# Third buffers for the first table and the rows, an eight-step pause and a larger side budget in the expert stage of a hybrid mLSTM, S5 and PEER block

## The chip, the cores and the metric

The kernel runs on one core of one Trainium2 chip. The metric is the device time of one execution in microseconds. Engines are PE (TensorE, matrix products), DVE (VectorE), ACT (ScalarE), POOL (GpSimd, which here issues the indirect gathers) and SP (SyncE, which issues the direct DMAs).

## The reference, cut to what matters

One block on 512 tokens of width 2048: an mLSTM and S5 mixer, and then the part that this change touches, the PEER layer. Each token has 8 heads with 16 experts each out of 16384. Both tables are 16384 x 2048 in float32:

```
ue = jnp.take(u_tab, it, axis=0)
ve = jnp.take(v_tab, it, axis=0)
act = gelu(einsum('td,ted->te', xt, ue))
out = einsum('te,ted->td', gt * act, ve)
```

`it` are the 128 experts of a token, `gt` their gates. All is float32.

## The kernel before, in words

The mixer, the second norm and the routing (queries, top 16, gates) take the first part. The expert layer is then computed in two ways at once.

**The dense part.** 72 blocks of 128 experts (28 fixed ones, 44 made of the most used experts) are multiplied with all 512 tokens. The first table is worked in 288 steps of the loop over `units`, four a block. A step n (`h_step`) does three things: `u_unit` transposes a quarter of a block three steps ahead (PE, L1482, into one of three PSUM tiles `tu`) and copies it to `uh` (ACT, L1484); `u_low` subtracts, two steps ahead, to get the low part `ul` (DVE, L1492); `h_unit` makes 12 matrix products of 512 columns (L115 to L117). After every fourth step a Gelu on ACT (L1504) writes `hg`, and SP stores it to DRAM (L1505). The block's table rows `ur` are loaded two blocks ahead: by SP for the first 28 blocks, by an indirect gather on POOL for the other 44 (L1051). I call these 288 steps the first stage. The second stage works the second table in 2 x 72 units: `hgl` (the stored activations) times the gates `gt` on DVE (L1546), both split in high and low parts (ACT L111, DVE L112), and 24 products of 512 columns a unit into eight PSUM banks. The gates come into play only in the first 72 units.

**The rows.** What the 72 blocks don't cover is done row by row: 147 jobs for each table. A job gathers one row of the table for each of 128 tokens into `gr` (POOL, L1346, 128 x 2048) and DVE makes one pass over it: a product with sum against the tokens `xa` (`mac_u`, L1343) for the first table, a scaled addition (`mac_v`, L1350) for the second. `xa` is loaded anew for each group of tokens, that is before jobs 0, 54, 90 and 121 of a table. All 294 jobs run in order.

**The gates.** `gbuild` makes the gate matrix in eight chunks of 64 tokens. A chunk is eight items; an item is five DVE operations (one-hot `go` tiles, L1069 and L1447) and, one item later, 24 small products on PE (L1435) whose sums ACT copies to the one tile `Gb` (L1436). After a chunk SP stores `Gb` with four DMAs of 1 MB in pieces of 256 bytes (L1456). `Gb` has one buffer, so the next chunk's first copy waits until the store has landed.

**The order.** All queues are in the order in which the code is run once. In the first stage each step adds `UBUD` to a budget, and side work is issued while the budget is positive: an item counts 3.45, a row job 2.5. Items come when they are due by a linear pace (64 items up to step 262), but not within `hold` steps after a chunk's store; otherwise a row job comes. Row jobs have `gr` tiles gathered two jobs ahead (the pool `rp` has two buffers) in the first stage, four ahead in the second, where the pool `rp2` adds two. In the second stage the remaining row jobs are spread evenly up to 14 units before the end. The chunks' stores come at the steps 127, 146, 166, 185, 204, 224, 243 and 262.

Of the kernel before, what the change touches and what calls it, by code (L numbers as in the profile page):

```python
# [8 lines left out]
F32 = mybir.dt.float32  # L9
F32R = mybir.dt.float32r  # L10
I32 = mybir.dt.int32
U32 = mybir.dt.uint32
BF16 = mybir.dt.bfloat16
AF = mybir.ActivationFunctionType
OP = mybir.AluOpType
# [4 lines left out]
P = 128  # L20
T = 512
D = 2048
# [6 lines left out]
NF = 28  # L29
NSEL = 44  # L30
NT = NF + NSEL
JN = P - NF
# [1 line left out]
RW = 64  # L34
SB = (54, 36, 31, 26)
JUNK = F32
UBUD = 2.8
GEND = 262
VPRE = 276
VEND = 14  # L40


# [5 lines left out]
def hybrid_block(ctx: ExitStack, tc: tile.TileContext, x, norm1_g, w_in, b_gates, conv_w, mnorm_g,  # L48
# [3 lines left out]
    v, s, g, pe, sp = nc.vector, nc.scalar, nc.gpsimd, nc.tensor, nc.sync  # L52
# [3 lines left out]
    def pool(name, bufs, side="left"):  # L56
        return tc.tile_pool(name=name, bufs=bufs, side=side, reuse_waits="tile")
# [37 lines left out]
    with pool(name="tmp", bufs=1, side="right") as tmp:  # L95
# [8 lines left out]
        p = tp_bank([P, 96])  # L104
# [749 lines left out]
    front.close()  # L854

    pk = ctx.enter_context(pool(name="pk", bufs=1, side="right"))
    subT = pk.tile([P, 2, P], F32, name="subT")
    iotaF = pk.tile([P, P], F32, name="iotaF")
    pcol = pk.tile([P, 1], F32, name="pcol")
    jt = pk.tile([P, P, 2], BF16, name="jt")  # L860
# [4 lines left out]
    DT = pk.tile([P, 5, T], BF16, name="DT")  # L865
# [2 lines left out]
    esel2 = pk.tile([P, 2, NSEL], I32, name="esel2")  # L868
    rl = pk.tile([P, TB, 2 * RW + 1], I32, name="rl")
    flag = pk.tile([P, 1], I32, name="flag")  # L870

    xn_d = dram.tile([T, D], F32, name="xn_d")
    gt_d = dram.tile([P * P, T], F32, name="gt_d")
# [43 lines left out]
    with pool(name="n2", bufs=1) as n2:  # L917
# [18 lines left out]
        p = tp_bank([P, 2, P])  # L936
# [6 lines left out]
        v.tensor_copy(jt, iotaF[:, :, None].to_broadcast([P, P, 2]))  # L943
        v.tensor_scalar(tri, iotaF, pcol, None, op0=OP.is_gt)
    mix.close()
    ixs = ExitStack()
    ix = ixs.enter_context(pool(name="ix", bufs=1, side="right"))
    i1T, i2T, gT = (ix.tile([P, T], F32, name=n) for n in ("i1T", "i2T", "gT"))
    tks = ExitStack()
    tk = tks.enter_context(pool(name="tk", bufs=1, side="right"))  # L950
    gate = tk.tile([P, TB, P], F32, name="gate")
# [79 lines left out]
    for h in range(8):  # L1031
# [7 lines left out]
        for a in range(2):  # L1039
            p = tp_bank([P, TB, P])  # L1040
# [7 lines left out]
    UT = {}  # L1048
# [23 lines left out]
    def spread(row, n):  # L1072
        r = row.rearrange("p (a b) -> p a b", b=2)
        return r[:, :, None, :].to_broadcast([P, r.shape[1], n, 2])

    def select():
# [24 lines left out]
        c = ck.tile([P, JN], F32, name="c")  # L1101
        v.tensor_scalar(c, cnt, float(CLIP), None, op0=OP.min)
        oha = ck.tile([P, JN, P], BF16, name="oha")
# [9 lines left out]
        p = tp_bank([P, CLIP])  # L1113
# [4 lines left out]
        k = ck.tile([P, 2, CLIP], F32, name="k")  # L1118
# [37 lines left out]
        ab = ck.tile([P, 2, JN], F32, name="ab")  # L1156
        v.tensor_copy(ab, sli[:, 1:3])
        yield
        ohv = ck.tile([P, JN, 2, NSEL], BF16, name="ohv")
        for j in range(0, JN, 20):  # L1160
            js = slice(j, j + 20)
            v.tensor_tensor(oha[:, js], ab[:, 1, js, None].to_broadcast([P, 20, P]),
                            iotaF[:, None, :].to_broadcast([P, 20, P]), op=OP.is_equal)
            yield
            v.tensor_tensor(ohv[:, js, 1], ab[:, 0, js, None].to_broadcast([P, 20, NSEL]),
                            iotaF[:, None, 1:NSEL + 1].to_broadcast([P, 20, NSEL]), op=OP.is_equal)
            v.tensor_tensor(ohv[:, js, 0], ohv[:, js, 1],
                            iotaF[:, NF + j:NF + j + 20, None].to_broadcast([P, 20, NSEL]), op=OP.mult)
            v.tensor_scalar(ohv[:, js, 1], ohv[:, js, 1], pcol, None, op0=OP.mult)
            yield  # L1170
        p = tp_bank([P, 2, NSEL])
# [151 lines left out]

    def gr_tile():
        UT["n"] = UT.get("n", -1) + 1
        pl = UT["rp2"] if "rp2" in UT and UT["n"] % 4 > 1 else UT["rp"]
        t = pl.tile([P, D], F32, name="gr", bufs=2)
        key = "r2" if "rp2" in UT and pl is UT["rp2"] else "r1"
        UT[key] = UT.get(key, 0) + 1
        if UT[key] <= 2:  # L1330
            v.memset(t, 0.0)
        return t

# [15 lines left out]
    def mac_v(t, a, acc):  # L1349
        v.scalar_tensor_tensor(acc, t, a, acc, op0=OP.mult, op1=OP.add)  # L1350
# [8 lines left out]
    rjobs = [(w, b, j) for w in range(2) for b in range(TB) for j in range(SB[b])]  # L1359

    def rare():
        q = []
        k = 0
        xa = nx = None
        for n, (w, b, j) in enumerate(rjobs):
            if n == 0 or nx is None and n + 6 < len(rjobs) and rjobs[n + 6][2] == 0 and "rp2" in UT:
                nx = xa_tile()
                gather(nx, h1_d if rjobs[min(n + 6, len(rjobs) - 1)][0] and n else xn_d, tokc(rjobs[n + 6][1] if n else b))
            if j == 0:
                if nx is None:  # L1370
                    nx = xa_tile()
                    gather(nx, h1_d if w else xn_d, tokc(b))
                xa, nx = nx, None
            while k < len(rjobs) and k < n + (4 if "rp2" in UT else 2):
                t = gr_tile()
                row_gather(t, rjobs[k][0], rl[:, rjobs[k][1], rjobs[k][2]:rjobs[k][2] + 1])
                q.append(t)
                k += 1
            t = q.pop(0)
            a = racts[:, b, j:j + 1]  # L1380
            if w:
                mac_v(t, a, xa)
            else:
                mac_u(t, xa, a)
            if j == SB[b] - 1:
                if w:
                    rare_out(b, xa)
                else:
                    rare_w(b, 0, SB[b], racts[:, b, 0:SB[b]])
            UT["rare_n"] = n + 1  # L1390
            yield 2.5
# [31 lines left out]
    def gbuild():  # L1423
        stk = ExitStack()
        gb = stk.enter_context(pool(name="gb", bufs=1, side="right"))
        GC = 64
        GN = 8

        def fill(Gb, o, t0):
            for t4 in range(0, GN, 4):  # L1430
                p = tp_bank([P, 4, P])
                for t in range(4):
                    a, c = divmod(t4 + t, 2)
                    for k in range(3):
                        pe.matmul(p[:, t, :], o[1][:, a, :, c], o[2 + k][:, a, :, c], start=k == 0, stop=k == 2)  # L1435
                s.activation(Gb[:, :, t0 + t4:t0 + t4 + 4], p.rearrange("p t i -> p i t"), AF.Copy)  # L1436

        gv = gt_d.rearrange("(i k) t -> k i t", k=P)
        todo = []
        for c in range(0, T, GC):  # L1440
            Gb = gb.tile([P, P, GC], F32, name="Gb")
            for t0 in range(c, c + GC, GN):
                o = [gb.tile([P, GN // 2, P, 2], BF16, name=f"go{i}", bufs=2) for i in range(5)]
                onehot(o[0], 0, P, i1b, t0, GN)
                onehot(o[1], 0, P, i2b, t0, GN)
                for k in range(3):
                    v.tensor_tensor(o[2 + k], o[0], spread(DT[:, 2 + k, t0:t0 + GN], P), op=OP.mult)  # L1447
                todo.append((Gb, o, t0 - c))
                UT["gb_n"] += 1
                yield 3.45  # L1450
                if len(todo) > 1:
                    fill(*todo.pop(0))
            while todo:
                fill(*todo.pop(0))
            for a in range(0, P, 32):
                sp.dma_start(gv[:, a:a + 32, c:c + GC], Gb[:, a:a + 32, :])  # L1456
            UT["hold"] = UT["step"] + 4
        stk.close()
        yield 0.1

    ustk = ExitStack()
    up = ustk.enter_context(pool(name="up", bufs=1))

    def u_load(i):
        ur = up.tile([P, D], F32, name="ur", bufs=2)
        if i < NF:
            sp.dma_start(ur, u2[i * P:(i + 1) * P, :])
        else:
            assert UT["sel"]
            gather(ur, u2, esel[:, i - NF:i - NF + 1])  # L1470
        UT["r", i] = ur
# [16 lines left out]

    def u_low(i, q):
        uh, p = UT.pop(("p", i, q))  # L1490
        ul = up.tile([P, 4, P], F32R, name="ul", bufs=4)
        v.tensor_tensor(ul, p, uh.bitcast(F32), op=OP.subtract)  # L1492
        UT["u", i, q] = (uh, ul)

    def h_unit(i, q):
        if q == 0:
            UT["h", i] = mm_bank()
        uh, ul = UT.pop(("u", i, q))
        for a in range(4):
            k = q * 4 + a  # L1500
            mm3(UT["h", i], uh[:, a, :], ul[:, a, :], xh[:, k, :], xl[:, k, :], k == 0, k == 15)
        if q == 3:
            hg = up.tile([P, T], F32, name="hg", bufs=2)
            s.activation(hg, UT.pop(("h", i)), AF.Gelu)  # L1504
            sp.dma_start(hg_d[i], hg)  # L1505

# [48 lines left out]
    for n, (i, q) in enumerate(units):  # L1555
        h_step(i, q)
        if n == VPRE:
            drain("a")
# [3 lines left out]
        UT["step"] = n  # L1562
        bud += UBUD if n0 is not None else 2.9
        while bud > 0:
            if n0 is None and not sides["a"]:
                n0 = n
                sides["a"].append(gbuild())
                sides["g"].append(rare())
            gb_next = n0 is None or n >= UT["hold"] and UT["gb_n"] * (GEND - n0) <= (n - n0) * (T // 8)
            c = pump1("a") if gb_next else 0  # L1570
            c = c or (pump1("g") if n0 is not None else 0)
# [69 lines left out]
    o = banks()  # L1641
    for n, (h, i) in enumerate(vunits):
        if n == NT:
            for k, b_ in enumerate(o):
                s.activation(F0[:, k // 2, (k % 2) * 512:(k % 2) * 512 + 512], b_, AF.Copy)
            o = banks()
# [21 lines left out]
    with tc.If(fl_v > 0):  # L1668
        rare_rest(fb)
        for tb in range(TB):  # L1670
            t = fb.tile([P, D], F32, name="rg")
# [44 lines left out]
```

## Time and profile before

| | |
|---|---|
| three runs | 3181.9, 3192.2 (median), 3195.4 us |
| the profiled execution | 3185.5 us, its span 3183.6 us |
| busy in the span | PE 92%, DVE 70%, ACT 31%, POOL 27% |
| first stage | from 1044 us to some 2275 us of the span |
| second stage, units 0 to 71 | about 2290 to 2763 us |
| second stage, units 72 to 143 | about 2763 to 3152 us |

Times in a row are microseconds from the span's start unless a column says otherwise. A matrix product of 512 columns starts every 0.23 us when the granted clock is full.

### The profile page before, as it was taken

The page shows a single profiled execution, that of the slowest core. Times are in us where ns is not written, and L with a number is a line of the kernel's source. Part 1 is how long each engine was busy: PE and PEld are TensorE (multiplying, and loading weights), DVE is VectorE, ACT ScalarE, POOL GpSimd, SP SyncE. Part 2 cuts the span into 40 slices and gives each one's busy share as a digit, 9 for nine tenths or more (in the row PEclk, how much of TensorE's full clock was granted, in tenths as well). Part 3 has the DMA queues.
Part 4 walks back from the last instruction along what each step waited for, and adds up shares of the span by engine and source line. Part 5 has one row for each costly group of instructions (what it writes and reads, how often), then busy time and mean ns, then how long its engine had stood idle before and what let it go on. Part 6 is the DMA issues. An engine that isn't in the chain of part 4 may idle for free. (4 is left out here: it accounts for less than half of the span.)

```text
span 3183.6 us, 44978 instructions
## 1 busy us (share of the span) xinstructions
PE 2926.7 (92%) x17540; PEld 2462.5 (77%) x17540; DVE 2226.3 (70%) x3665; ACT 978.8 (31%) x1491; POOL 848.9 (27%) x656
## 2 busy tenths in 40 slices
PE   7999999999799999998999998896698888899997
PEld 5888978899688887886777787775477666688886
DVE  7467544432388977874767876774688888889885
ACT  5343555432322321121222222221122222232223
POOL 3000111000200000001222222222244888647860
PEclk9999999999899999997999999998899999999999
DMA  4422444353322221634778667779899997999983
GB/s 142 129 87 85 102 108 119 105 175 133 134 87 86 100 95 67 242 140 147 258 241 283 181 193 241 252 245 323 296 395 381 403 401 240 407 408 406 394 328 134
DMA packets 366140, 691.92 MB, mean 217 GB/s; under 512 B 169490, under 2 KB 248850, under 8 KB 320338
## 3 DMA queue, kind: packets, MB, share of 16 engines
q0 software_dynamic: 74240, 393.57, 33.0%
q1 hardware_dynamic: 291680, 295.40, 28.2%
q8 instruction: 140, 2.29, 0.3%
q14 instruction: 80, 0.66, 0.1%
HBM read 644.04 MB, written 96.86 MB: 233 GB/s over the span
## 5 line engine op out<-in xcount | busy, mean ns | idle before, releaser
L115 PE MATMUL mm<-xh,uh 128*128 128x512 f32 x1152 | 494.6, 429 | 0.0
L117 PE MATMUL mm<-xh,ul 128*128 128x512 f32 x1152 | 465.1, 404 | 7.5 <-DVE ul L1492 7.5
L116 PE MATMUL mm<-xl,uh 128*128 128x512 f32 x1152 | 465.3, 404 | 0.0
L1343 DVE SCALAR_TENSOR_TENSOR junk<-gr,xa 128x2048 f32<-128x2048 f32 x147 | 335.8, 2284 | 163.0 <-DMA gr<-in_peer_u_dram,rl 149.0
L1350 DVE SCALAR_TENSOR_TENSOR xa<-gr,racts,xa 128x2048 f32<-128x2048 f32 x147 | 345.4, 2350 | 58.1 <-DMA gr<-in_peer_v_dram,rl 56.8
L112 DVE TENSOR_TENSOR wl<-wr,wh 128x1024 fp32r<-128x1024 f32 (+1 forms) x144 | 187.1, 1302 | 240.2 <-ACT wh L111 240.1
L1484 ACT ACTIVATE uh<-tu 128x512 fp32r<-128x512 f32 x288 | 171.6, 600 | 501.4 <-PE tu L1482 489.4
L1346 POOL DMA_INDIRECT gr<-in_peer_u_dram,rl x147 | 180.2, 1226 | 460.8 <-DVE junk L1343 419.1
L115 PE MATMUL mm<-wh,xh 128*128 128x256 f32 (+1 forms) x1024 | 294.6, 288 | 0.0
L117 PE MATMUL mm<-wh,xl 128*128 128x256 f32 (+1 forms) x1024 | 288.8, 282 | 1.8 <-DVE xl L112 1.8
L116 PE MATMUL mm<-wl,xh 128*128 128x256 f32 (+1 forms) x1024 | 289.0, 282 | 0.0
L116 PE MATMUL tp<-vl,ewh 128*128 128x512 f32 x576 | 232.5, 404 | 61.1 <-DVE vl L112 61.0
L1346 POOL DMA_INDIRECT gr<-in_peer_v_dram,rl x147 | 248.6, 1691 | 131.9 <-DVE xa L1350 83.3
L117 PEld LDWEIGHTS mm<-xh,ul 128*128 128x128 f32 x1152 | 225.7, 196 | 62.4 <-DVE ul L1492 8.7
L117 PE MATMUL mm<-xh,wl 128*128 128x512 f32 x640 | 255.9, 400 | 12.1 <-DVE wl L112 12.1
L111 ACT ACTIVATE ewh<-hgl 128x512 fp32r<-128x512 f32 x144 | 91.0, 632 | 561.4 <-DVE hgl L1546 275.9
L115 PE MATMUL mm<-xh,wh 128*128 128x512 f32 x640 | 258.3, 404 | 0.0
L116 PEld LDWEIGHTS mm<-xl,uh 128*128 128x128 f32 x1152 | 227.5, 197 | 39.6
L115 PEld LDWEIGHTS mm<-xh,uh 128*128 128x128 f32 x1152 | 227.1, 197 | 39.4
L116 PE MATMUL mm<-xl,wh 128*128 128x512 f32 x640 | 254.9, 398 | 0.0
L1482 PE MATMUL tu<-ident,ur 128*128 128x128 f32 x1152 | 182.1, 282 | 73.0 <-DVE ul L1492 72.3
L111 ACT ACTIVATE wh<-wr 128x1024 fp32r<-128x1024 f32 (+1 forms) x144 | 166.8, 1161 | 260.5 <-PE mm L117 103.0
(498 smaller groups left out, 6080.4 us busy)
## 6 DMA issues: line engine op xcount, KB each, us to landing
wr<-in_w_in_dram SPq DMA_DIRECT2D x80, 512.0 KB, 3.6
gt_d<-Gb SPq DMA_DIRECT2D x32, 1024.0 KB, 17.0
ur<-in_peer_u_dram SPq DMA_DIRECT2D x28, 1024.0 KB, 5.0
vr<-in_peer_v_dram SPq DMA_DIRECT2D x56, 512.0 KB, 14.9
hg_d<-hg SPq DMA_DIRECT2D x72, 256.0 KB, 2.2
hgl<-hg_d SPq DMA_DIRECT2D x72, 256.0 KB, 9.3
w_d<-hgl SPq DMA_DIRECT2D x72, 256.0 KB, 7.6
hgl<-w_d SPq DMA_DIRECT2D x72, 256.0 KB, 7.9
```

The lines of the kernel that those rows point to most:

```text
L111: s.activation(hi, src, AF.Copy)
L112: v.tensor_tensor(lo, src, hi.bitcast(F32), op=OP.subtract)
L115: pe.matmul(o, ah, bh, start=start, stop=False)
L116: pe.matmul(o, ah, bl, start=False, stop=False)
L117: pe.matmul(o, al, bh, start=False, stop=stop)
L1343: v.scalar_tensor_tensor(UT["junk"], t, 1.0, xg, op0=OP.mult, op1=OP.mult, accum_out=a)
L1346: g.indirect_dma_start(out=t, out_offset=None, in_=v2 if w else u2, in_offset=IOA(ap=col, axis=0), bounds_check=P * P - 1, oob_is_err=False)
L1350: v.scalar_tensor_tensor(acc, t, a, acc, op0=OP.mult, op1=OP.add)
L1482: pe.transpose(p[:, a, :], ur[:, k * P:(k + 1) * P], ident)
L1484: s.activation(uh, p, AF.Copy)
```

## The change

Six edits, all in the expert layer:

- `ur` (first table) has three buffers in place of two, still loaded two blocks ahead; `gr` has three in `rp` (jobs gathered three ahead, five ahead in the second stage, with `rp` and `rp2` taken 3 to 2).
- To make room, `ul` goes from four buffers to three, `hg` from two to one, the one-hot set `go` from five tiles to four (the third product is written over the one-hot tile), and the subkeys' tile lies in a pool that is freed earlier.
- `hold` after a chunk's store goes from 4 steps to 8.
- `UBUD` goes from 2.8 to 3.0.
- `GEND` and `VPRE` are written by the number of blocks; their values stay 262 and 276.
- The selection's loop may end in a shorter piece; with the sizes here it never does.

```
-UBUD = 2.8
-GEND = 262
-VPRE = 276
+UBUD = 3.0
+HOLD = 8
+GEND = 4 * NT - 26
+VPRE = 4 * NT - 12
...
-        pl = UT["rp2"] if "rp2" in UT and UT["n"] % 4 > 1 else UT["rp"]
-        t = pl.tile([P, D], F32, name="gr", bufs=2)
...
+        key = "rp2" if "rp2" in UT and UT["n"] % 5 > 2 else "rp"
+        nb = {"rp": 3, "rp2": 2}[key]
+        t = UT[key].tile([P, D], F32, name="gr", bufs=nb)
...
-            while k < len(rjobs) and k < n + (4 if "rp2" in UT else 2):
+            while k < len(rjobs) and k < n + (5 if "rp2" in UT else 3):
...
-                o = [gb.tile([P, GN // 2, P, 2], BF16, name=f"go{i}", bufs=2) for i in range(5)]
+                o = [gb.tile([P, GN // 2, P, 2], BF16, name=f"go{i}", bufs=2) for i in range(4)]
...
-                    v.tensor_tensor(o[2 + k], o[0], spread(DT[:, 2 + k, t0:t0 + GN], P), op=OP.mult)
+                    v.tensor_tensor(o[2 + k if k < 2 else 0], o[0], spread(DT[:, 2 + k, t0:t0 + GN], P), op=OP.mult)
...
-            UT["hold"] = UT["step"] + 4
+            UT["hold"] = UT["step"] + HOLD
...
-        ur = up.tile([P, D], F32, name="ur", bufs=2)
+        ur = up.tile([P, D], F32, name="ur", bufs=3)
...
-        ul = up.tile([P, 4, P], F32R, name="ul", bufs=4)
+        ul = up.tile([P, 4, P], F32R, name="ul", bufs=3)
...
-            hg = up.tile([P, T], F32, name="hg", bufs=2)
+            hg = up.tile([P, T], F32, name="hg")
```

On DVE, in the pause after the store of step 146, three row jobs stood between the `ul` subtractions before the next chunk's first one-hot tile (`go`):

```order
L1492 TENSOR_TENSOR ul<-tu,uh 128x512
L1343 SCALAR_TENSOR_TENSOR junk,racts<-gr,xa 128x2048
L1492 TENSOR_TENSOR ul<-tu,uh 128x512
L1343 SCALAR_TENSOR_TENSOR junk,racts<-gr,xa 128x2048
L1492 TENSOR_TENSOR ul<-tu,uh 128x512
L1343 SCALAR_TENSOR_TENSOR junk,racts<-gr,xa 128x2048
L1492 TENSOR_TENSOR ul<-tu,uh 128x512
L1069 TENSOR_TENSOR go_16176<-jt,i1b 128x1024
```

Now eight do; these are the last six of them:

```order
L1346 SCALAR_TENSOR_TENSOR junk,racts<-gr,xa 128x2048 x2
L1495 TENSOR_TENSOR ul<-tu,uh 128x512
L1346 SCALAR_TENSOR_TENSOR junk,racts<-gr,xa 128x2048
L1495 TENSOR_TENSOR ul<-tu,uh 128x512
L1346 SCALAR_TENSOR_TENSOR junk,racts<-gr,xa 128x2048
L1495 TENSOR_TENSOR ul<-tu,uh 128x512
L1346 SCALAR_TENSOR_TENSOR junk,racts<-gr,xa 128x2048
L1495 TENSOR_TENSOR ul<-tu,uh 128x512
L1346 SCALAR_TENSOR_TENSOR junk,racts<-gr,xa 128x2048
L1495 TENSOR_TENSOR ul<-tu,uh 128x512
L1071 TENSOR_TENSOR go_16294<-jt,i1b 128x1024
```

What moved: the one-hot work of the next chunk lies four steps later, and five more row jobs lie ahead of it. The chunk still ends at the same step.

On POOL, at the end of the first stage and over into the second, the gathers of rows (`gr`), of table blocks (`ur`) and of tokens (`xa`) stood like this:

```order
L1346 DMA gr<-in_peer_u_dram,rl 128x2048 x2
L1051 DMA xa<-xn_d,rl 128x2048
L1346 DMA gr<-in_peer_u_dram,rl 128x2048 x2
L1051 DMA ur<-in_peer_u_dram,esel 128x2048
L1346 DMA gr<-in_peer_u_dram,rl 128x2048 x5
L1051 DMA ur<-in_peer_u_dram,esel 128x2048
L1346 DMA gr<-in_peer_u_dram,rl 128x2048 x4
L1051 DMA ur<-in_peer_u_dram,esel 128x2048
L1346 DMA gr<-in_peer_u_dram,rl 128x2048 x14
L1051 DMA xa<-xn_d,rl 128x2048
L1346 DMA gr<-in_peer_u_dram,rl 128x2048 x28
```

And now:

```order
L1349 DMA gr<-in_peer_u_dram,rl 128x2048 x3
L1053 DMA ur<-in_peer_u_dram,esel 128x2048
L1349 DMA gr<-in_peer_u_dram,rl 128x2048 x5
L1053 DMA ur<-in_peer_u_dram,esel 128x2048
L1349 DMA gr<-in_peer_u_dram,rl 128x2048 x5
L1053 DMA ur<-in_peer_u_dram,esel 128x2048
L1349 DMA gr<-in_peer_u_dram,rl 128x2048 x5
L1053 DMA ur<-in_peer_u_dram,esel 128x2048
L1349 DMA gr<-in_peer_u_dram,rl 128x2048 x6
L1053 DMA xa<-xn_d,rl 128x2048
L1349 DMA gr<-in_peer_u_dram,rl 128x2048 x22
```

What moved: the last load of `xa` for the first table (job 121) lay past the end of the first stage, where `xa` has a second buffer, and lies now six rows behind the last block's gather. Counted over the whole order, DVE has done 115 of the 147 first-table jobs when it comes to the first split of the second stage, and now 129.

## Rows read from the trace of the kernel before

**Rows 1.** Busy time by stage: PE, PEld, DVE, ACT, POOL, PEclk, DMA share, GB/s
```profile
1490.00:2143.60 653.60, 598.43 (x3974) 498.95 (x3975) 480.20 (x645) 179.68 (x320) 153.91 (x125) 0.96 0.72 237
2143.60:2290.00 146.40, 93.02 (x384) 72.11 (x382) 79.99 (x84) 18.07 (x32) 38.87 (x35) 0.82 0.88 307
2290.00:2763.00 473.00, 412.26 (x1705) 326.23 (x1705) 392.91 (x345) 117.17 (x149) 322.10 (x190) 0.97 0.95 367
2763.00:3152.00 389.00, 388.32 (x1702) 321.32 (x1703) 329.83 (x236) 121.88 (x157) 222.10 (x133) 0.99 0.89 355
```
**Rows 2.** DMA queues from 2290 to 2763 us: q0 carries POOL's gathers
```profile
q0 software_dynamic: 24384, 117.01, 63.6%
```
**Rows 3.** Waits from 2290 to 2763 us: total, times, longest
```profile
PE tp L116 <- DVE vl L112: 57.3, 36, 5.4
```
**Rows 4.** Waits from 1490 to 2143.6 us
```profile
POOL ur L1051 <- PE tu L1482: 227.2, 35, 19.6
...
ACT Gb L1436 <- DMA gt_d<-Gb: 100.0, 7, 27.0
...
PE tu L1482 <- DVE ul L1492: 35.5, 13, 10.2
PE tp L1435 <- ACT Gb L1436: 25.9, 4, 9.9
```
**Rows 5.** PE in order of time, 1925 to 1932 us
```profile
1927.43 1.44 PE L1435 MATMUL tp<-go,go 128*128 128x128 bf16 x12 [9.87 <-ACT Gb L1436]
...
1930.48 0.63 PE L116 MATMUL mm<-xl,uh 128*128 128x512 f32 x1
1930.91 0.63 PE L117 MATMUL mm<-xh,ul 128*128 128x512 f32 x1
```
**Rows 6.** SP's queue, 1656 to 1692 us, after the store of step 146
```profile
1656.30 19.17 SPq L1456 DMA_DIRECT2D gt_d<-Gb  x4
1675.56 15.39 SPq L1505 DMA_DIRECT2D hg_d<-hg  x3
```
**Rows 7.** ACT in the same stretch
```profile
1658.88 0.60 ACT L1504 ACTIVATE hg<-mm 128x512 f32<-128x512 f32 x1 [2.12 <-PE mm L117]
...
1662.49 0.60 ACT L1484 ACTIVATE uh<-tu 128x512 fp32r<-128x512 f32 x1 [2.52 <-PE tu L1482]
...
1671.69 0.60 ACT L1504 ACTIVATE hg<-mm 128x512 f32<-128x512 f32 x1 [2.17 <-PE mm L117]
1681.11 1.09 ACT L1436 ACTIVATE Gb<-tp 128x512 f32<-128x512 f32 x2 [8.81 <-DMA gt_d<-Gb]
```
**Rows 8.** DMA issues, 1675.5 to 1678 us: KB each, us to landing
```profile
hg_d<-hg SPq DMA_DIRECT2D x1, 256.0 KB, 12.2
```
**Rows 9.** DMA queues, 1656 to 1690 us: q1 carries SP's transfers
```profile
q1 hardware_dynamic: 16736, 4.72, 58.4%
q0 software_dynamic: 918, 6.61, 49.2%
```
**Rows 10.** SP's queue after the store of step 204
```profile
1886.12 29.45 SPq L1456 DMA_DIRECT2D gt_d<-Gb  x4
1915.67 3.49 SPq L1505 DMA_DIRECT2D hg_d<-hg  x1
```
**Rows 11.** DMA issues, 1915 to 1916 us
```profile
hg_d<-hg SPq DMA_DIRECT2D x1, 256.0 KB, 11.6
```
**Rows 12.** Waits from 2143.6 to 2290 us
```profile
DVE junk L1343 <- DMA gr<-in_peer_u_dram,rl: 57.7, 21, 7.3
...
PE tu L1482 <- DVE ul L1492: 36.2, 10, 8.2
...
DVE junk L1343 <- DMA xa<-xn_d,rl: 8.3, 1, 8.3
```
**Rows 13.** DVE in order of time, 2184 to 2188 us
```profile
2184.79 2.29 DVE L1343 SCALAR_TENSOR_TENSOR junk<-gr,xa 128x2048 f32<-128x2048 f32 x1 [4.94 <-DMA gr<-in_peer_u_dram,rl]
...
2187.01 0.68 DVE L1492 TENSOR_TENSOR ul<-tu,uh 128x512 fp32r<-128x512 f32 x1
```

More of the change, by code (lines that the diff above doesn't have):

```diff
@@ L856, in hybrid_block @@
     pk = ctx.enter_context(pool(name="pk", bufs=1, side="right"))
-    subT = pk.tile([P, 2, P], F32, name="subT")
     iotaF = pk.tile([P, P], F32, name="iotaF")
@@ L870, in hybrid_block @@
     flag = pk.tile([P, 1], I32, name="flag")
+    ixs = ExitStack()
+    ix = ixs.enter_context(pool(name="ix", bufs=1, side="right"))
+    i1T, i2T, gT = (ix.tile([P, T], F32, name=n) for n in ("i1T", "i2T", "gT"))
+    subT = ix.tile([P, 2, P], F32, name="subT")
     xn_d = dram.tile([T, D], F32, name="xn_d")
@@ L945, in hybrid_block @@
     mix.close()
-    ixs = ExitStack()
-    ix = ixs.enter_context(pool(name="ix", bufs=1, side="right"))
-    i1T, i2T, gT = (ix.tile([P, T], F32, name=n) for n in ("i1T", "i2T", "gT"))
     tks = ExitStack()
@@ L1160, in select @@
         for j in range(0, JN, 20):
-            js = slice(j, j + 20)
-            v.tensor_tensor(oha[:, js], ab[:, 1, js, None].to_broadcast([P, 20, P]),
-                            iotaF[:, None, :].to_broadcast([P, 20, P]), op=OP.is_equal)
+            m = min(20, JN - j)
+            js = slice(j, j + m)
+            v.tensor_tensor(oha[:, js], ab[:, 1, js, None].to_broadcast([P, m, P]),
+                            iotaF[:, None, :].to_broadcast([P, m, P]), op=OP.is_equal)
             yield
-            v.tensor_tensor(ohv[:, js, 1], ab[:, 0, js, None].to_broadcast([P, 20, NSEL]),
-                            iotaF[:, None, 1:NSEL + 1].to_broadcast([P, 20, NSEL]), op=OP.is_equal)
+            v.tensor_tensor(ohv[:, js, 1], ab[:, 0, js, None].to_broadcast([P, m, NSEL]),
+                            iotaF[:, None, 1:NSEL + 1].to_broadcast([P, m, NSEL]), op=OP.is_equal)
             v.tensor_tensor(ohv[:, js, 0], ohv[:, js, 1],
-                            iotaF[:, NF + j:NF + j + 20, None].to_broadcast([P, 20, NSEL]), op=OP.mult)
+                            iotaF[:, NF + j:NF + j + m, None].to_broadcast([P, m, NSEL]), op=OP.mult)
             v.tensor_scalar(ohv[:, js, 1], ohv[:, js, 1], pcol, None, op0=OP.mult)
@@ L1325, in gr_tile @@
         UT["n"] = UT.get("n", -1) + 1
-        pl = UT["rp2"] if "rp2" in UT and UT["n"] % 4 > 1 else UT["rp"]
-        t = pl.tile([P, D], F32, name="gr", bufs=2)
-        key = "r2" if "rp2" in UT and pl is UT["rp2"] else "r1"
-        UT[key] = UT.get(key, 0) + 1
-        if UT[key] <= 2:
+        key = "rp2" if "rp2" in UT and UT["n"] % 5 > 2 else "rp"
+        nb = {"rp": 3, "rp2": 2}[key]
+        t = UT[key].tile([P, D], F32, name="gr", bufs=nb)
+        UT["c" + key] = UT.get("c" + key, 0) + 1
+        if UT["c" + key] <= nb:
             v.memset(t, 0.0)
@@ L1434, in fill @@
                     for k in range(3):
-                        pe.matmul(p[:, t, :], o[1][:, a, :, c], o[2 + k][:, a, :, c], start=k == 0, stop=k == 2)
+                        pe.matmul(p[:, t, :], o[1][:, a, :, c], o[2 + k if k < 2 else 0][:, a, :, c], start=k == 0, stop=k == 2)
                 s.activation(Gb[:, :, t0 + t4:t0 + t4 + 4], p.rearrange("p t i -> p i t"), AF.Copy)
```

## The prediction

> **What bounds the kernel now.** I read the busy times by stage first, then the waits of each stage, then single stretches in order of time.
>
> From unit 72 of the second stage on PE is busy 388.3 of 389 us at full clock: nothing in this change can shorten that part [rows 1]. The first 72 units have the same products and take 473 us, 84 more, with the DMA engines at 0.95 of their time [rows 1]. The 57.3 us in which PE waits there for DVE's splits [rows 3] are late rows passed on: DVE is in order, and a late `gr` holds up the split behind it. So this part is bound by transfers.
>
> In the first stage PE is the busiest (598 of 654 us), and the DMA engines are at 0.72 [rows 1]. What PE loses there are two waits: 35.5 us for `ul` from DVE, of which one of 10.2 us belongs to the rows' first start, and 25.9 us in four waits for the copy to `Gb`, which itself waited 100 us, seven times, for the chunk's store to land [rows 4]. After a long wait the clock is down: behind the 9.87 us one, products start 0.43 us apart in place of 0.23, which is the 1.2 GHz level, 0.2 us more for each; I count 2 us for a restart, ten products [rows 5]. In the last 26 steps (2143.6 to 2290 us) there is no gate work left; PE waits 36.2 us for `ul` and the mean clock is 0.82 [rows 1, 12]. There DVE waits 57.7 us, 21 times, for a row [rows 12].
>
> **The change part by part.** The sum is made against the profiled execution, 3185.5 us (2 us of it around the span), which is 6.7 us under the median of the three runs; the forecast is given against the median.
>
> *Rows taken out of the second stage.* By the order, DVE has done 115 row jobs when the second stage starts, and now 129. By the 72nd unit it is 211 and now 217, so that stretch carries 88 jobs for 96. A row is 128 x 2048 x 4 bytes, 1.05 MB. The gathers' queue takes 63.6% of 473 us, 301 us, for 117 MB [rows 2]: 2.57 us a MB, 2.7 a row. 8 x 2.7 is 21.6 us of a transfer time that is full; by DVE's time it would be 8 x 2.29 = 18 [rows 13]. I take -20. The ends are 0 (the rows weren't what was late) and -57 (two more buffers in the mix take all of PE's waits away). The six rows that leave the units from 72 on give nothing: PE is full there.
>
> *The eight-step pause.* The chunk's store now has nine or ten steps until the next copy, not five or six. At 3.2 us a step (two Gelus, four steps apart, are 12.8 us apart [rows 7]) that is 29 to 32 us. After step 146 the store had landed 24.8 us after its start, when the copy went on [rows 6, 7]; after step 204 only 41 us after it [rows 5, 10]. So most of the 25.9 us goes, with 5 us of slow clock, and I leave 6 us for late stores: -25, between -10 and -31. What is late next in the pause is the next two terms.
>
> *Third buffers.* POOL waited 227 us, 35 times, to put a `ur` gather behind the transposes that read its buffer [rows 4], and row gathers queued behind it. With three buffers this wait is gone, and a row has two jobs of lead in place of one. Against it stands a denser pause: eight jobs in eight steps, where it was three in four. While a store is under way the two queues share the engines, 58.4% and 49.2%, and the gathers get 6.6 MB in 34 us [rows 9]. Eight jobs, three of them already in buffers, and one or two `ur` are 6 to 7.5 MB: just what fits. Of the 25 us of waits for `ul` that lie in the pauses I take 8 off; the ends are -25 and +15.
>
> Rows 9 show about equal shares with two row buffers already. The Trainium skill (DMA: Bandwidth & Descriptors, section Queues, rings and completion order) says that each DMA engine goes round its queues, a packet at a time. The trace's shares agree; by that rule a third row in flight earns the gathers no larger share beside a store, this term is 0, and the sum would be 8 us less of a gain.
>
> *One `hg` buffer: the added wait.* A Gelu must now wait until the last one's store has landed, and on SP that store is queued behind the chunk's four. After step 146 the next Gelu came 2.6 us after the store's start, its own store was issued at 1675.56 and landed 12.2 us later, 31.5 us after the start [rows 6 to 8]. The second Gelu, at 15.4 us, had a second buffer; now ACT stands for 16 us. Behind it on ACT is the copy `uh`, on DVE the subtraction behind that and the row jobs. PE can run three more steps (9.6 us), and after the release it needs Gelu, copy and subtraction, 0.6 + 0.6 + 0.7 [rows 7, 13]: PE loses what is over about 7.5 us. By the step at which a chunk ends, the first Gelu comes one step later (146, 166, 262), two (185), three (204, 224) or four (127, 243). With landing at 31.5 that is 3 x 8.6 + 5.4 + 2 x 2.2 + 0 = 36 us. After step 204 the store was issued at 1915.67 and landed 11.6 us later, 41.2 us after the start [rows 10, 11]; if all were so late, it is 3 x 18.3 + 15.1 + 2 x 11.9 + 2 x 8.7 = 111. If all land by 20 us it is 0. I take +38, the nearer row and a little slow clock, because part of it lies in the waits for rows above.
>
> *The last 26 steps.* With two buffers a row is asked for when the one before last is done, and DVE waits 2.7 us a row [rows 12]. Three buffers let the transfers run on, at 0.88 of their time so far [rows 1]: 0.88 x 146 is 129 us of work, and a row more than before makes 132, so at 0.97 the stretch takes 136 us, -10. It contains the load of `xa` for job 121, which costs about what the one there now did (8.3 us of DVE [rows 12]); that one moves up into the pause after step 243. I take -10, between -44 (all PE waits) and +12.
>
> *The rest.* A third clearing of a row buffer on DVE is 2 us at most; `ul` with three buffers ties DVE to two steps of lead, which matters only where PE waits anyway; the product over the one-hot tile makes its next writer wait for PE where the second tile's writer, the next operation, did before, under PE's work. +2.
>
> Sum: -20 - 25 - 8 + 38 - 10 + 2 = -23, 3162 for the profiled execution and 3169 for the median.
>
> **The rivals.**
>
> *The `hg` store is late everywhere (slower).* One mechanism: each pause's second Gelu waits behind the chunk's store. For it: more rows in flight beside the store make it land later, and the row after step 204 shows 41 us. Against it: most stores had the queue free sooner. At 41 us the term is 111 and eight slow restarts of 2 us, 127 in place of 38: 3169 + 89 = 3258 at worst. At 37 us the same working gives 3 x 14.1 + 10.9 + 2 x 7.7 + 2 x 4.5 = 78 and some 14 of clock, +54: 3223. From a landing at about 34 us on the kernel is slower than before, from 36 us on by more than 0.5%.
>
> *The rows move, and nothing is won (no change).* The first stage pays 14 x 2.7 = 38 us of transfers for what the second saves. For it: in the pauses the engines are full [rows 9]. Against it: 0.72 on the whole [rows 1], so four fifths would have to fall where it is full. The gain of the third buffers and of the last steps is gone (+18): 3187.
>
> *Prefetch clears the first stage (much faster).* The row waits (-25), the `Gb` waits (-31) and half of the last stretch's (-22) go, the Gelu's wait is 20 and the second stage gains 25: -83, 3109. For it speaks that PE is the only engine near full there [rows 1]; against it the pauses' transfers [rows 9].
>
> **How the numbers follow.** About 0.5%, 16 us, is what a measurement of this kernel can tell from no change. Chances: the forecast 0.45, with 3145 to 3190 as its own range; no change 0.2; late `hg` 0.18; much faster 0.17. Of the forecast's case about three quarters lie under 3176, which with the much faster case and a little of the no-change case makes 0.53 for faster; 0.29 within; 0.18 slower. The range takes in the much faster case and the slower one up to a landing at 36 us: 3108 to 3214.
>
> **What would show it.** Right: the stretch of the first 72 units near 450 us, with 88 row jobs; no PE wait on L1435 over 3 us; POOL's wait of `ur` on transposes gone; a new wait of the Gelu for a DMA from `hg`, in most pauses, of up to 16 us, and a PE wait for `ul` behind it; the last 26 steps under 140 us. The forecast is wrong if the Gelu doesn't wait (then faster), if the stores land later than 36 us after the chunk's start (then slower), or if the first 72 units stay near 470 us.

## The result, and the profile after

| | before | changed | ratio |
|---|---|---|---|
| time, median (15 runs each) | 3186.4 us | 3202.1 us | 1.0051 [1.0040, 1.0061] |
| profiled execution, its span | 3185.5, 3183.6 us | 3199.9, 3198.1 us | |

The kernel became slower by half a per cent, where the forecast was 3169 us and faster. The time by stage, in the same columns as [rows 1]:

```profile
1490.00:2190.50 700.50, 601.16 (x3974) 501.20 (x3975) 514.68 (x671) 179.43 (x321) 173.43 (x139) 0.92 0.70 238
2190.50:2326.20 135.70, 89.03 (x383) 69.75 (x382) 84.25 (x88) 18.03 (x33) 44.93 (x36) 0.85 0.92 327
2326.20:2782.00 455.80, 414.29 (x1721) 332.56 (x1722) 378.87 (x326) 119.00 (x148) 305.02 (x183) 0.95 0.96 374
2782.00:3168.00 386.00, 384.39 (x1693) 317.21 (x1692) 312.64 (x226) 119.53 (x157) 200.62 (x124) 1.00 0.86 336
```

Read it line against line: the last 26 steps take 135.7 us for 146.4, the first 72 units of the second stage 455.8 for 473, the rest hardly moves. Only the first line is longer: the steps from 1490 us to the last chunk's store take 700.5 us for 653.6, and the mean clock in them falls from 0.96 to 0.92. So 47 us were lost where the gates are built, and some 31 won behind.

The waits of the changed kernel in that first stretch (total, times, longest), which answer to [rows 4]:

```profile
ACT hg L1507 <- DMA hg_d<-hg: 154.2, 6, 32.1
...
PE tu L1485 <- DVE ul L1495: 71.3, 12, 20.7
POOL ur L1053 <- PE tu L1485: 62.1, 10, 26.6
...
DVE junk L1346 <- DMA gr<-in_peer_u_dram,rl: 42.4, 18, 10.6
...
PE tp L1438 <- ACT Gb L1439: 35.8, 3, 14.9
DVE junk L1346 <- DMA xa<-xn_d,rl: 22.0, 2, 11.3
```

ACT no longer waits for the chunk's store; a new wait stands in its place, the Gelu for the landing of the last `hg` store, up to 32 us. PE's wait for `ul` has doubled. PE still waits 35.8 us for copies to `Gb`, now because these are queued on ACT behind the Gelu: each of the three waits ends some 2 us after a Gelu that had waited 26 to 32 us. One pause shows the chain: SP's queue after the store of step 146, then ACT, DVE and PE of the same moment (answers to [rows 6, 7]).

```profile
1654.15 38.38 SPq L1459 DMA_DIRECT2D gt_d<-Gb  x4
1692.62 15.02 SPq L1508 DMA_DIRECT2D hg_d<-hg  x3
```
```profile
1698.81 0.60 ACT L1507 ACTIVATE hg<-mm 128x512 f32<-128x512 f32 x1 [32.07 <-DMA hg_d<-hg]
...
1699.92 0.69 DVE L1495 TENSOR_TENSOR ul<-tu,uh 128x512 fp32r<-128x512 f32 x1 [19.72 <-ACT uh L1487]
...
1700.67 1.12 PE L1485 MATMUL tu<-ident,ur 128*128 128x128 f32 x4 [20.73 <-DVE ul L1495]
```

The chunk's four DMAs hold SP's queue for 38.4 us in place of 19.2, the `hg` store goes out behind them and lands 44.7 us after the chunk's start (31.5 before), and PE stands for 20.7 us. The queues in the 30 us from that start (packets, MB, share) show what took its place: the gathers now move 8.1 MB and the store 2.5, where it was 5.4 and 4.5 before.

```profile
q0 software_dynamic: 1117, 8.10, 69.9%
q1 hardware_dynamic: 9940, 2.54, 37.2%
```

As a mean over the eight stores it was 5.2 MB of gathers to 4.0 of SP's transfers before, and is 7.1 to 3.2.

### The profile page after: what moved, and what is told of

Same layout as the page of the kernel before. It is cut to its first block, busy times and chain, and to the rows that moved or that the text cites. A ratio compares the mean times of both kernels' runs of the same rounds, so it can differ in the third digit from the quotient of the medians.

```text
span 3198.1 us, 45174 instructions
## 1 busy us (share of the span) xinstructions
PE 2921.0 (91%) x17540; PEld 2461.6 (77%) x17540; DVE 2236.1 (70%) x3666; ACT 977.7 (31%) x1491; POOL 839.0 (26%) x656
## 5 line engine op out<-in xcount | busy, mean ns | idle before, releaser
L1349 POOL DMA_INDIRECT gr<-in_peer_u_dram,rl x147 | 187.6, 1276 | 590.7 <-DVE junk L1346 522.5
L1495 DVE TENSOR_TENSOR ul<-tu,uh 128x512 fp32r<-128x512 f32 x288 | 196.4, 684 | 132.8 <-ACT uh L1487 96.4
```

Source lines behind the costliest of these rows:

```text
L1349: g.indirect_dma_start(out=t, out_offset=None, in_=v2 if w else u2, in_offset=IOA(ap=col, axis=0), bounds_check=P * P - 1, oob_is_err=False)
```

## The experiments

Each run gives the median time and its ratio to the kernel before, with a 95% interval of 0.0010 to 0.0021 to either side. Runs are compared by their ratios; a difference of 0.01 is 32 us, and one under about 0.002 is hardly to be told from nothing. "A chunk" is the time from the second chunk store's start to the eighth's, divided by six: 81.2 us before, 89.4 in the changed kernel. Theory 1 was that the late `hg` store costs the time; theory 2, that the third row buffer takes the transfers' share from the chunk's store; and later a third, that the long pause bunches the row jobs onto the time of that store.

**Two `hg` buffers.** In the changed kernel (two small tiles were moved to another pool for room):

```
-            hg = up.tile([P, T], F32, name="hg")
+            hg = up.tile([P, T], F32, name="hg", bufs=2)
```

> The changed kernel with two hg buffers again (two small constant tiles move to a pool that is freed earlier, to make the room). Theory 1, the single hg buffer: the Gelu's 185.5 us of waits for the store of hg go to under 5, PE's waits for ul and for the Gb copy, 110.7 and 35.8 us, fall to some 50 in all, and the time to 3140 us (3110 to 3165). Rival, the pause is full of transfers and something must wait: the chunk's store still lands some 40 us after its start, the same loss shows as waits for rows and for Gb, and the time stays within 3190 to 3205 us.

3187.0 us, 1.0003 [0.9990, 1.0016]; a chunk 85.9 us. The Gelu's waits fall from 185.5 to 52.2 us (from 1480 us to the second stage), and the buffer is worth 0.0048, 15 us; the time lies between the two forecasts. So the wait is real, but with it nearly gone the kernel is no faster than before: theory 1 explains a part only, and the first `hg` store after a chunk is still issued up to 45 us late.

**One `hg` buffer in the kernel before**, the opposite edit.

> The kernel before with one hg buffer and nothing else changed. Theory 1: the Gelu waits for the hg store in most pauses, 60 to 100 us in all since the stores land 23 to 41 us after the chunk's start there, PE loses some 36 us, partly in place of its waits for the Gb copy: 3205 to 3225 us. Rival (full transfers in the longer pause): the buffer alone costs nothing, 3180 to 3193 us.

3190.3 us, 1.0009 [0.9996, 1.0023]: some 3 us, hardly to be told from nothing. The Gelu waits 54.2 us in three waits, and PE hardly notices (72.8 us for `ul`, 71.7 before). One buffer costs only where the store is late.

**The `hg` store from ACT's queue**, with one buffer:

```
-            sp.dma_start(hg_d[i], hg)
+            s.dma_start(hg_d[i], hg)
```

> The changed kernel with its one hg buffer, but hg is stored from ACT's queue in place of SP's, so it isn't queued behind the chunk's store. Theory 1 in the form that the queue's order makes the store late: the Gelu's waits fall from 185 to under 30 us, and the time comes to within 15 us of the run with two buffers. Rival in the form that the DMA engines themselves are full: the small store lands late from any queue, the Gelu still waits 100 us or more in all, and less than 20 us are gained.

3186.4 us, 0.9999 [0.9983, 1.0016]: the Gelu's waits for the store are gone and the time is that of two buffers. So it was the place behind the chunk on SP's queue that made the store late, and not the store itself. The copies to `Gb` wait for the chunk's store again (89.6 us on ACT), and PE 54.3 us for them.

**Two row buffers** in the changed kernel (`nb = 2`, jobs gathered two and four ahead):

> The changed kernel with two row buffers and two jobs of lead as before (four in the second stage); one hg buffer, eight-step pause, budget 3.0 and the third ur buffer stay. Theory 2, the share: more row gathers in flight take the DMA engines from the chunk's store; with two, the gathers move 5 to 6 MB in the 30 us after a store's start in place of 7.1, the stores land some 10 us sooner, the Gelu's waits fall from 185 to 60 to 120 us, and the time to 3175 to 3195 us in spite of more waits for rows. Rival, the budget: the rows asked for in the pause are the same eight, so the store is as late, the Gelu waits 160 us or more, rows come later besides, 3200 to 3220 us.

3222.9 us, 1.0101 [1.0080, 1.0121]. Theory 2 had the transfers right: gathers 5.5 MB and SP 4.1 in the 30 us, the `hg` store issued 11 to 28 us after the chunk (11 to 45 with three). It had the time wrong: DVE's waits for rows go up from 67.7 to 184.3 us and PE's for `ul` from 110.7 to 139.1. The third row buffer slows the store and is still worth 0.0050, 16 us.

**The budget back to 2.8:**

```
-UBUD = 3.0
+UBUD = 2.8
```

> The changed kernel with the budget of 2.8: some 14 row jobs go back to the second stage. Theory 2: the pause still has three rows in flight, so the store stays late: the Gelu waits 120 us or more, the first stage ends 10 to 25 us sooner than in the changed kernel, the second stage is 20 us longer, 3195 to 3210 us in all. Rival, the budget is what hurts: the Gelu's waits fall under 80 us and the time to 3175 to 3188 us.

3212.7 us, 1.0071 [1.0052, 1.0090]: slower than either forecast. The larger budget is a gain of 0.0020, some 6 us, if anything. It isn't what made the kernel slower.

**A pause of four steps** in the changed kernel:

```
-HOLD = 8
+HOLD = 4
```

> The changed kernel with the pause of four steps. Theory 1: the second Gelu still meets the store, its waits fall from 185 to 80 to 130 us since fewer rows run beside the store, and PE waits for the Gb copy again; 3190 to 3205 us. Rival (it is the rows packed into the pause): the stores land within 32 us, and the time falls to 3160 to 3175 us.

3182.2 us, 0.9987 [0.9977, 0.9997], 0.0064 or 20 us better than with eight, between the two forecasts; a chunk 85.3 us. PE waits 72.9 us for the copy to `Gb` now, and only 53.3 for `ul`.

**Four steps and two `hg` buffers.**

> Two hg buffers and the pause of four steps, the rest of the change as it is. Theory 1 and 2 together: the Gelu hardly waits, fewer rows beside the store; PE waits for the Gb copy stay at 60 to 80 us; 3165 to 3182 us. Rival, the pause's length doesn't matter once hg has two buffers: 3183 to 3192 us as with eight steps.

3172.7 us, 0.9953 [0.9936, 0.9969]; a chunk 84.2 us. With two `hg` buffers the pause costs 0.0050, 16 us, so the most of its price is not the `hg` store's.

**Eight steps, two `hg` buffers, and rows asked for one job less ahead inside a pause:**

```
-k < n + (5 if "rp2" in UT else 3)
+k < n + (5 if "rp2" in UT else 3 - (UT["step"] < UT["hold"]))
```

> Two hg buffers, the pause of eight steps, and within the pause rows are asked for only two jobs ahead in place of three. Theory 2: the store keeps its share and lands within 35 us, PE's waits for the Gb copy (42.6 us in the run with two hg buffers) fall under 20, those for ul rise by less; 3155 to 3175 us. Rival: the rows are then late by as much as the store is sooner; 3180 to 3192 us.

3177.1 us, 0.9969 [0.9955, 0.9982], 0.0034 better than two `hg` buffers alone, between the two forecasts. The gathers' part in the 30 us did not fall (7.1 MB), and the Gelu's waits stay (54.7 us); PE's waits for `ul` are 73.4 us for 80.3. A gain, but not by way of the share that the edit was to change; how it comes about stays open.

**The pause alone.** The kernel before, and nothing changed but the pause:

```
-            UT["hold"] = UT["step"] + 4
+            UT["hold"] = UT["step"] + 8
```

> The kernel before with nothing changed but the pause, eight steps in place of four (two row buffers, two hg buffers, budget 2.8). Bunching theory: the row jobs crowd onto the time of the chunk store and the DMA engines idle in the catch-up, so it is 6 to 20 us slower than before (ratio 1.002 to 1.006); the copy to Gb waits less for the store (under 70 us on ACT in place of 100), and the row waits of DVE in the gate steps grow. Theory of the prediction: PE's 25.9 us of waits for the copy go and nothing takes their place: 15 to 25 us faster (0.992 to 0.995).

3218.0 us, 1.0108 [1.0089, 1.0128]: 34 us slower, more than the whole change. Both theories had less or the other sign. Its waits from 1480 us to the second stage:

```profile
DVE junk L1343 <- DMA gr<-in_peer_u_dram,rl: 200.9, 64, 12.2
...
PE tu L1482 <- DVE ul L1492: 115.7, 35, 10.8
```

In the kernel before, the same two are:

```profile
DVE junk L1343 <- DMA gr<-in_peer_u_dram,rl: 145.2, 38, 11.6
...
PE tu L1482 <- DVE ul L1492: 71.7, 23, 10.2
```

The wait of PE for the copy to `Gb` is gone from the list, as the forecast had it; 44 us of waits for `ul` have come instead. The stretch up to the last chunk's store, which answers to the first of [rows 1], is 33 us longer:

```profile
1490.00:2176.81 686.81, 610.51 (x3974) 505.00 (x3975) 483.15 (x646) 183.12 (x320) 160.90 (x126) 0.94 0.68 226
```

PE's waits in it are 81.3 us, all for `ul`, where they were 61.4 in all, and PE is busy 12 us longer with as many instructions at a mean clock of 0.94 in place of 0.96. DVE in the pause after step 146 shows the waits arise: a row that isn't there, and behind it the subtraction.

```profile
1663.32 0.68 DVE L1492 TENSOR_TENSOR ul<-tu,uh 128x512 fp32r<-128x512 f32 x1
1672.82 2.29 DVE L1343 SCALAR_TENSOR_TENSOR junk<-gr,xa 128x2048 f32<-128x2048 f32 x1 [8.82 <-DMA gr<-in_peer_u_dram,rl]
...
1675.04 0.69 DVE L1492 TENSOR_TENSOR ul<-tu,uh 128x512 fp32r<-128x512 f32 x1
```

Two stretches of this chunk, in the columns of [rows 1]: the 42 us from the store on, and the rest up to the next store.

```profile
1657.29:1699.29 42.00, 30.90 (x133) 24.66 (x132) 22.35 (x23) 6.33 (x11) 10.29 (x9) 0.83 1.04 328
1699.29:1749.38 50.09, 50.09 (x382) 42.28 (x382) 38.99 (x61) 17.33 (x31) 10.16 (x7) 0.97 0.48 174
```

And the same chunk of the kernel before:

```profile
1656.30:1698.30 42.00, 39.19 (x244) 31.80 (x243) 30.29 (x41) 11.08 (x20) 10.45 (x9) 1.00 1.02 323
1698.30:1735.09 36.79, 36.79 (x272) 31.15 (x271) 30.66 (x43) 12.16 (x22) 10.85 (x7) 1.00 0.67 244
```

In the 42 us the DMA engines are full in both (328 and 323 GB/s), but PE does 133 matrix instructions in place of 244, at a lower clock; then PE is full, and the DMA engines stand idle for half of the time. The work of one resource has been gathered in one place and that of the other in the next. The store itself isn't late: its four DMAs hold SP's queue for 19.3 us after step 146, 19.2 before.

**The same pause, rows paced.** The last kernel with a budget of 1.6 a step inside a pause and 3.6 outside; the first stage has the same 115 row jobs:

```
-        bud += UBUD if n0 is not None else 2.9
+        bud += 2.9 if n0 is None else UBUD if not UT["hold"] else 1.6 if n < UT["hold"] else 3.6 if n < GEND else UBUD
```

> The kernel before with the eight-step pause, and the budget paced: 1.6 a step inside a pause and 3.6 outside it (2.8 throughout in the eight-step run), so that a pause carries five or six row jobs in place of eight or nine and the steps behind it more; the 115 row jobs of the first stage are the same number. Bunching theory: the 32 us that the eight-step pause cost come back for the greater part, 3180 to 3200, with DVE's row waits back under 170 us from 200.9 and PE's waits for ul under 90 from 115.7. Rival, the pause costs by itself (the gate items crowded behind it, whatever the rows do): 3210 to 3225.

3190.6 us, 1.0014 [1.0000, 1.0028]: 0.0094 or 30 us come back; a chunk 82.0 us, 86.6 with the pause unpaced. Its waits from 1480 us to the second stage:

```profile
DVE junk L1343 <- DMA gr<-in_peer_u_dram,rl: 189.5, 54, 12.2
...
PE tu L1482 <- DVE ul L1492: 75.5, 29, 10.8
...
PE tp L1435 <- ACT Gb L1436: 15.0, 4, 6.1
```

DVE's waits for rows hardly fell, which the forecast had wrong, but PE's for `ul` did: most late rows no longer hold up a subtraction that PE needs. The same stretches:

```profile
1650.64:1692.64 42.00, 37.54 (x219) 30.64 (x217) 27.77 (x38) 9.78 (x18) 11.04 (x8) 1.00 1.09 334
1692.64:1735.80 43.16, 40.12 (x295) 33.39 (x295) 32.48 (x42) 13.25 (x24) 11.61 (x8) 0.96 0.58 211
```

219 matrix instructions beside the store, for 133, and full clock. In these 42 us DVE makes five row passes; unpaced it made eight, and six in the kernel before. The rival is out: with the larger budget behind the pause the gate items stand at least as close together here, and the time is back all the same. So the third theory holds: what the pause costs is the row jobs that the program's budget puts into it, not the eight steps. It holds as an order of work on DVE. It doesn't hold as a matter of transfers, since the gathers in the 30 us from a store's start moved 6.1 MB as a mean here and 5.4 unpaced.

Even paced, the long pause gains nothing over the short one. Up to the last chunk's store PE waits 15.0 us for the copy to `Gb`, 25.9 before, but 44.7 us for `ul`, 35.5 before.

**A pause of two steps, with two `hg` buffers.**

> The changed kernel with two hg buffers and a pause of two steps in place of eight. Bunching theory, if it goes on below four steps: PE's waits for the copy to Gb grow (over 85 us, where the four-step pause with two hg buffers had 67.9), its waits for ul fall further (under 50 us), and the sum is 0 to 8 us faster than the four-step version, 3165 to 3173. Rival: four steps is about the best, since the copy waits for the store either way: 3 to 15 us slower than the four-step version, 3176 to 3188.

3171.1 us, 0.9958 [0.9945, 0.9972]: the same as four steps, with 69.2 us of PE's waits for the copy in place of 67.9. The gain ends at four; the time is still within what the first of the two had, but the copy's waits didn't grow as it had it.

**A budget of 3.2**, four steps, two `hg` buffers.

> The four-step version with two hg buffers and a budget of 3.2 in place of 3.0. If side work moved ahead still pays as from 2.8 to 3.0 (some 10 us): 3160 to 3167, the second stage starting 10 to 20 us later and its first 72 units being 25 us shorter. Rival, the first stage is full of transfers: it ends later by what the second saves, 3170 to 3182.

3187.6 us, 1.0016 [1.0002, 1.0030], 20 us slower than with 3.0. The second stage starts at 2323.3 us for 2294.4 and its first 72 units take 443.2 us for 453.5: 29 paid and 10 saved. The direction was the rival's; the loss is past its range.

**Two `ur` buffers** in the changed kernel:

```
-        ur = up.tile([P, D], F32, name="ur", bufs=3)
+        ur = up.tile([P, D], F32, name="ur", bufs=2)
```

> The changed kernel with two ur buffers in place of three. By the prediction's term, POOL's wait of the ur gathers for PE's transposes (62 us in the changed kernel) goes back over 200 us and holds the row gathers queued behind it: 5 to 12 us slower than the changed kernel (3207 to 3214). Rival: with three row buffers the rows have lead enough to ride over a late ur, and the third ur buffer only puts one more gather beside the chunk store: within 4 us of the changed kernel, or faster (3190 to 3205).

3188.8 us, 1.0018 [1.0003, 1.0033]: 0.0033 or 11 us faster than with three, though POOL's wait for PE's transposes goes from 62.4 back to 239.3 us. That wait cost nothing that shows. The third buffer only moved it: from 1480 us to the second stage, POOL's waits before a row gather, for DVE to release a `gr` buffer, are 482.4 us with three `ur` buffers,

```profile
POOL gr L1349 <- DVE junk L1346: 482.4, 82, 37.6
```

and with two they are 266.8:

```profile
POOL gr L1349 <- DVE junk L1346: 266.8, 68, 19.5
POOL ur L1053 <- PE tu L1485: 239.3, 26, 25.1
```

**Two `ur` buffers, two `hg` buffers, four steps.**

> The four-step version with two hg buffers, and two ur buffers in place of three. If the third ur buffer costs by one more gather beside each chunk store whatever the pause is: 5 to 15 us faster than that version (3172.7), 3158 to 3168. If it cost only because the eight-step pause was full: within 5 us, 3168 to 3178. If the third buffer does help the row gathers once the pause is short: 3178 to 3190.

3160.1 us, 0.9914 [0.9897, 0.9932]: faster than both kernels, and 0.0039 or 12 us better than with three `ur` buffers. So the third one costs in a short pause too. With the pause, `hg` and `ur` as they were before, what is left of the change is worth 27 us; what the fewer `ul` and `go` tiles cost in it was not tried. Its waits from 1480 us to the second stage:

```profile
POOL ur L1053 <- PE tu L1485: 184.5, 31, 23.2
ACT Gb L1439 <- DMA gt_d<-Gb: 125.0, 7, 23.7
...
PE tu L1485 <- DVE ul L1495: 56.6, 17, 12.6
...
PE tp L1438 <- ACT Gb L1439: 49.1, 6, 12.1
```

With three `ur` buffers ACT's copies waited 138.7 us for the store, and PE 67.9 us for the copy to `Gb` and 50.4 for `ul`. So the copy waits less for the store. That the early gather of `ur` delays the store is argued from this, not shown; the gathers' part in the 30 us is 6.5 MB with either.

## Why the prediction was wrong

*Right: rows out of the second stage.* Forecast -20; from PE's first product to the first copy out of PSUM in the middle, 2290.26 to 2764.93 us became 2326.21 to 2781.92: -19. Only half of it is the working's, so the size is in part luck: DVE makes seven row passes fewer there (92 for 99), but the gathers' queue moves 113.9 MB for 117.0 [rows 2], 3 MB less and not the 8 of eight rows, and the rest is a rate of 374 GB/s for 367 [rows 1]. PE's waits for DVE's splits fall from 57.3 us [rows 3] to 39.9, and those for ACT's from 10.0 to 7.0:

```profile
PE tp L117 <- DVE vl L113: 39.9, 21, 5.8
...
PE tp L116 <- ACT vh L112: 7.0, 1, 7.0
```

*Right in size: the last 26 steps.* Forecast -10, at 136 us; measured 146.4 to 135.7. The DMA engines come to 0.92 of their time, not to the working's 0.97. DVE waits there 25.3 us for rows, 57.7 before [rows 12], as the working had it. PE got little of that: its waits for `ul`, 43.7 us before (36.2 [rows 12] and 7.5 before products), are 39.5, and half of these are one wait behind a Gelu that waited for its buffer. The rest of the 10.7 us is PE's busy time, 89.0 us for 93.0, and waits that no line names:

```profile
PE tu L1485 <- DVE ul L1495: 39.5, 9, 18.6
ACT hg L1507 <- DMA hg_d<-hg: 31.3, 1, 31.3
DVE junk L1346 <- DMA gr<-in_peer_u_dram,rl: 25.3, 18, 3.9
```

*Wrong, and the main cause: the eight-step pause.* The prediction put it at -25, between -10 and -31; alone it is +34, and in the changed kernel 16 (two `hg` buffers) to 20 us (one). That the waits for the copy go came true with the pause alone; in the changed kernel they stand at 35.8 us, behind the Gelu. The step that failed is the sentence that eight jobs, with the `ur` gathers, are "just what fits". It compared MB with the 34 us of a store [rows 9], not with the time of the eight steps: by its own figures 6 to 7.5 MB take 31 to 39 us, and eight steps of 3.2 us are 26. It left out that every job in the pause stands on DVE ahead of a subtraction that PE needs, so that the steps wait for the rows, and that the steps that gave up their jobs leave the DMA engines at 0.48. No bound on the side of a loss was given to this term, though the next one named a denser pause; that was the mistake, since no row showed a pause of eight jobs. The rival "rows move, nothing is won" looked at the transfers as a sum of 38 us; what mattered was where the row jobs stand, as the paced run shows with the same pause and the same 115 jobs.

*Third buffers: the sum near, the parts not.* Forecast -8. The third row buffer is worth 16 us and the third `ur` buffer costs 11, together -5 as differences, so that the sum is near by luck. That the wait of POOL for the transposes, the largest of [rows 4], was worth something is refuted by the two-`ur` runs. Refuted too is that a third row in flight earns no larger share beside a store. The rule cited from the Trainium skill (DMA: Bandwidth & Descriptors, section Queues, rings and completion order) was read as equal shares of time. In packets [rows 9] had 16736 against 918 as the profile counts them, which no equal round gives if both queues have work throughout; whether they had is not shown, so the rule itself is neither borne out nor refuted here. What refutes the inference is that two row buffers gave the gathers 5.5 MB to SP's 4.1 in 30 us, and three 7.1 to 3.2. The measurement decides.

*One `hg` buffer: the wait larger, its price smaller.* Forecast 38 us with landing at 31.5 us. The landing was 44.7 after step 146. The prediction had such landings as its slower rival, with 111 us for 41; the kernel did become slower, but not for that price: measured were 15 us with eight steps, 11 with four (0.9987 to 0.9953) and 3 in the kernel before. The waits don't add: the Gelu's 185 us give PE 30 more of waits for `ul` than with two buffers (110.7 and 80.3). That PE would have waited for rows in most of that time anyway is likely, but not shown.

*The rest.* The larger budget is what moves the rows of the first term; what they cost in the first stage had no term. With 2.8, in the traces, the second stage to the end is 20 us longer (892.2 us for 871.9) and the first ends 6 us sooner. The differences of single edits don't sum to the +16 of the change; that most of them act on the same wait is argued from this: +34 for the pause was measured with two row buffers, with three it is 16 to 20.

## What to carry over

A pause for one kind of work is filled with another: before it is lengthened, count what the planner will issue in it, step by step, on the engine and on the queue, compare it with the time of those steps, and pace it. A long wait of an engine that isn't late costs nothing, however large it stands in the list: taking away 177 of POOL's 239 us made the kernel slower. Sum waits that end in the same engine as one, by the place where they fall, and bound a term to the side of a loss wherever the trace doesn't show the density that it makes.

## What was not expected of the hardware

The store in pieces of 256 bytes got less of the DMA engines when more gathers were in flight. From two row buffers to three, with rows of 8 KB, SP's transfers in the 30 us from its start fell from 4.1 to 3.2 MB as a mean, and the gathers' rose from 5.5 to 7.1. A chunk is 4.2 MB, so at 4.1 it had mostly landed. In the densest pause of the changed kernel, after 2012.35 us, it was 1.93 MB against 9.36:

```profile
q0 software_dynamic: 1286, 9.36, 76.8%
q1 hardware_dynamic: 7553, 1.93, 28.3%
```

That is 1286 packets against 7553: shares equal neither in packets nor in bytes. The number of buffers isn't all that decides, for the paced run with its two had 3.5 MB against 6.1.
